# Input tiles stored tile-major and rope tables packed, with the tiles' loads queued behind slabs that they no longer block

## The chip, the cores and the metric

The kernel runs on the 8 cores of one Trainium2 chip, one batch element per core, with no traffic between cores. The time is device microseconds of the slowest core, lower is better. Executions fall into a fast and a slow state: in a slow run the cores of one die, or of both, show a lower granted TensorE clock (about 0.97 is usual) and take longer.

## The reference, cut to what matters

Four layers of a diffusion backbone over 2048 latent tokens and 256 context tokens, width 1024. Only the beginning matters: layer 0 normalises the input, modulates it by shift and scale vectors that come from one vector of conditioning, and feeds the pooling and attention mixer.

```python
for l in range(DEPTH):
    mod = silu_c @ w_mod[l] + b_mod[l]                  # 1024 x 6144: twelve slabs of 512 columns
    sh1, sc1, g1, sh2, sc2, g2 = [m[:, None, :] for m in jnp.split(mod, 6, axis=-1)]
    ...
    hx = modulate(rms_norm(x, norm1_g[l]), sh1, sc1)    # needs slabs 0 to 3
    if l % 2 == 0:
        ...                                             # k, v, q (rotated by the rope tables), pooling input u
        out_x, out_c = even_mixer(hx, hc, ...)
    else:
        ...                                             # conformer convolution
    x = x + g1 * out_x                                  # needs slabs 4 and 5
    x = x + g2 * sq_relu_mlp(modulate(rms_norm(x, norm2_g[l]), sh2, sc2), mlp_w1[l], mlp_w2[l])
    ...                                                 # slabs 6 to 11; the context stream likewise
```

## The kernel before

The tokens are worked on in five tiles: tiles 0 to 3 of 512 latent tokens, tile 4 with the 256 context tokens. The residual stream X stays in SBUF as float32, channels on partitions. Weights come in slabs of 1024 rows or columns through four slots (`WR`), loaded from the POOL queue, which also casts float32 to bfloat16 (a modulation slab's rows are 16 KB in the input, its packets in the trace 8192 B); the input tiles and rope tables are loaded from the SP queue, without a cast. Every engine's program is a list made at build time; each instruction waits for the semaphores of what it reads and of what it overwrites.

```python
X = SB("X", [128, 8, NT], F32)            # channel-major: the 512 tokens of one chunk of 128 channels, then the next
...
def dmas(self, qname, chan, pairs, reads=(), writes=()):
    q = self.E[qname]
    self._emit_waits(q, self._deps(chan, reads, writes))
    for (out, in_) in pairs:
        chan.count += 16
        q.q.append(("op", "dma_start", (), {"out": out, "in_": in_}, chan.sem, 16))
    self._record(chan, chan.count, reads, writes)       # a reader of a slot: the slot's next load waits for it
...
def load_x(tile, after=()):
    (t0, n, s, ti) = tile
    Sd.dma("sp", Sd.chan("x%d" % ti), X[:, :, t0:t0 + n],
           xP[:, 8 * t0:8 * (t0 + n)].rearrange("p (c t) -> p c t", c=8), reads=after, writes=xk(ti))
...
def pump():                               # loads the next slabs of the plan into slots that are free
    while slabs["free"] and slabs["next"] < len(plan):
        i = slabs["next"]
        slot = slabs["free"].pop(0)
        src, nk = plan[i]
        Sd.dma("pool", Sd.chan("w%d" % slot), WR[slot][:, 0:src.shape[1]], src, writes=[("W", slot)])
        ...
```

So that the tiles do not all load at once, a tile's load names a modulation slab in `reads`: it is issued when that slab has landed. A side effect is that the slot counts as read by the tile's transfer, and that the slot's next slab is not loaded before the tile has landed. The start of the program, and the part of the mixer where layer 0's slabs are used:

```python
X5 = x_tiles(True)
load_x(X5[0])
mods = [get_slab(w_mod[0, j], 8) for j in range(4)]
Sd.dma("pool", Sd.chan("ident"), IDB[:, :], identd, writes=[("c", "idb")])
first_mixer = even_mixer(0, X5, ...)      # issues rope table 0, X tile 1 behind slab 2, table 1, tile 2 behind slab 3,
                                          # table 2, tile 3, table 3, tile 4; two DMAs to a table, cosine and sine
for j in range(4):
    mod_slab(0, j, mods[j])               # 32 matmuls, then the slot is given back; from j = 1 on also tile 0's norm
    ...
for tile in X5[1:]:
    push_norm(0, 0, tile, ...)            # squares, statistics and pieces, run a few at a time between other work
...
kvs = get_slab(w_kv[i2], 8); qs_ = get_slab(w_q[i2], 8); us_ = get_slab(w_u[i2], 8)
kv_tile(all5[0], kvs, ...)                # key and value of tile 0
kv_tile(all5[1], kvs, ...)                # of tile 1, once its norm is done
for f in q_items(0, qs_):                 # queries of tile 0, with tile 2's norm between them
    f(); step(2)
kv_tile(all5[2], kvs, ...)
for b in range(4):
    u_item(b, us_); step(3)
mod_slab(0, 4)                            # then tile 3, slab 5, tile 4, slab 6; slabs 7 to 11 in the first attention
...
```

The softmax here doesn't subtract the row's maximum and nothing guards it: scores larger than these inputs give would overflow.

Of the kernel before, what the change touches and what calls it, by code (L numbers as in the profile page):

```python
# [14 lines left out]
NT = S + L  # L15
# [18 lines left out]
class Sched:  # L34
# [86 lines left out]

    def dma(self, qname, chan, out, in_, reads=(), writes=()):
        self.dmas(qname, chan, [(out, in_)], reads, writes)

    def dmas(self, qname, chan, pairs, reads=(), writes=()):
        if self.dry:
            return
        q = self.E[qname]
        self._emit_waits(q, self._deps(chan, reads, writes))
        for (out, in_) in pairs:  # L130
            chan.count += 16
            q.q.append(("op", "dma_start", (), {"out": out, "in_": in_}, chan.sem, 16))
        self._record(chan, chan.count, reads, writes)
# [108 lines left out]
def build():  # L242
# [22 lines left out]
    masksd = din("masks", [128, 2 * 128])  # L265
    ropec = din("ropec", [128, NT])
    ropes = din("ropes", [128, NT])
    permd = din("permc", [128, 128])
# [3 lines left out]
    with ExitStack() as st:  # L272
        def SB(name, shape, dt):
            return st.enter_context(nc.sbuf_tensor(name, shape, dt))

        X = SB("X", [128, 8, NT], F32)
        H = SB("H", [128, 8, NT], BF16)
# [26 lines left out]
        def emit(Sd, plan):  # L304
            dry = Sd.dry
            A = Arena(ART, ARENA_W, Sd)
            psk = lambda i: ("ps", i)
            hk = lambda ti: [("H", ti, c) for c in range(8)]
            xk = lambda ti: [("X", ti, c) for c in range(8)]

# [74 lines left out]
            def load_x(tile, after=()):  # L385
                (t0, n, s, ti) = tile
                Sd.dma("sp", Sd.chan("x%d" % ti), X[:, :, t0:t0 + n], xP[:, 8 * t0:8 * (t0 + n)].rearrange("p (c t) -> p c t", c=8),
                       reads=after, writes=xk(ti))

# [38 lines left out]
            def norm_sq(tile, c, k=2):  # L428
                (t0, n, s, ti) = tile
                ACT(H[:, c:c + k, t0:t0 + n], X[:, c:c + k, t0:t0 + n], AF.Square, [("X", ti, q) for q in range(c, c + k)],  # L430
                    [("H", ti, q) for q in range(c, c + k)])
# [12 lines left out]
            def norm_piece(lb, nrm, tile, r, c, mode="da"):  # L444
                (t0, n, s, ti) = tile
                tb = c % 2
                rst, rk, ak = RST[:, r, 0:n], ("rst", r), ("ab", lb, nrm, c // 2)
                tmp, x, h = TMP[:, tb, 0:n], X[:, c, t0:t0 + n], H[:, c, t0:t0 + n]
                if mode == "da":
# [23 lines left out]
            def push_final(tile, outb, sq=True):  # L473
# [8 lines left out]
                def piece(c):  # L482
                    STT(ob[:, c, 0:n], X[:, c, t0:t0 + n], vec("fing", c, c + 1), RST[:, r, 0:n], ALU.mult, ALU.mult,
                        [("X", ti, c), ("rst", r)] + VK, [ok[c]])
                    if c % 2:
                        Sd.dma("sp", Sd.chan("o%d%d" % (ti % 2, c // 2)), outP[:, 8 * t0 + (c - 1) * n:8 * t0 + (c + 1) * n].rearrange("p (c t) -> p c t", c=2),
                               ob[:, c - 1:c + 1, 0:n], reads=ok[c - 1:c + 1])
# [3 lines left out]
            def mlp_phase(l, tiles, next_l, next_tiles):  # L491
# [25 lines left out]
                def stage2(w2s, it, last):  # L517
                    (t0, n, s, ti) = tiles[it]
                    hb, hbk = hid[it % 2]
                    for oc in range(8):  # L520
                        pb = dbank()
                        for kk in range(4):
                            MM(PS[pb][:, 0:n], w2s[0][:, kk, oc * 128:(oc + 1) * 128], hb[:, kk, 0:n], kk == 0, kk == 3,
                               reads=[w2s[1], hbk[kk]], writes=[psk(pb)], last=(kk == 3))
                        STT(X[:, oc, t0:t0 + n], PS[pb][:, 0:n], gate(1, oc, s), X[:, oc, t0:t0 + n], ALU.mult, ALU.add,
                            [psk(pb), gkey(1, oc), ("X", ti, oc)], [("X", ti, oc)])
                        if last and ti in next_ti and oc % 2:
                            norm_sq(tiles[it], oc - 1)
                        step()
# [24 lines left out]
            def proj_item(slabs_, tile, oc):  # L554
# [3 lines left out]
                for k in range(8):  # L558
                    MM(PS[pb][:, 0:n], sl[0][:, k, (oc % 4) * 128:(oc % 4 + 1) * 128], H[:, k, t0:t0 + n], k == 0, k == 7,
                       reads=[sl[1], ("H", ti, k)], writes=[psk(pb)], last=(k == 7))  # L560
                STT(X[:, oc, t0:t0 + n], PS[pb][:, 0:n], gate(0, oc, s), X[:, oc, t0:t0 + n], ALU.mult, ALU.add,
                    [psk(pb), gkey(0, oc), ("X", ti, oc)], [("X", ti, oc)])
# [165 lines left out]

            def even_mixer(l, tiles, loads=()):
                i2 = l // 2  # L730
# [7 lines left out]
                Qs = [A.bf16("Qs%d" % i, 4, 512, parts=4) for i in range(2)]  # L738
                Us = [A.bf16("Us%d" % i, 512) for i in range(NU_)]
                Pb = [A.bf16("P%d" % i, 1024) for i in range(NP)]  # L740
                Db = [A.bf16("Db%d" % i, 512) for i in range(2)]
                BND, Bk = A.bf16("BND", 20, 128)
                MSK, Mk = A.bf16("MSK", 2, 128)
                PW, PWk = A.bf16("PW", 4, 128)
                RT = [(A.f32("rc%d" % i, 512), A.f32("rs%d" % i, 512)) for i in range(2)]
                t1, t1k = A.f32("t1", 512)
# [12 lines left out]
                def rope_buf(i):  # L759
                    if i < 2:  # L760
                        return RT[i]
                    return tuple((Pb[2 * i - 4 + j][0].bitcast(F32), Pb[2 * i - 4 + j][1]) for j in range(2))

                def load_rope(ti, i):
                    t0, n = all5[ti][0:2]
                    (rc, rck), (rs, rsk) = rope_buf(i)
                    Sd.dmas("sp", Sd.chan("rt%d" % i), [(rc[:, 0:n], ropec[:, t0:t0 + n]), (rs[:, 0:n], ropes[:, t0:t0 + n])], writes=rck + rsk)

                def rope_a(pq, tab, n):
                    (rc, rck), (rs, rsk) = tab  # L770
                    ub = UB[cnt["u"] % 2]
                    cnt["u"] += 1
                    TT(t1[:, 0:n], PS[pq][:, 0:n], rc[:, 0:n], ALU.mult, [psk(pq)] + rck, t1k)
                    TT(ub[0][:, 0:n], PS[pq][:, 0:n], rs[:, 0:n], ALU.mult, [psk(pq)] + rsk, ub[1])
                    return ub
# [155 lines left out]
                def even_run():  # L931
# [3 lines left out]
                    qs_ = get_slab(w_q[i2], 8)  # L935
                    us_ = get_slab(w_u[i2], 8)
                    Sd.dma("pool", Sd.chan("c0"), BND[:, :, :], bandsd.rearrange("p (a b) -> p a b", a=20), writes=Bk)
                    Sd.dma("pool", Sd.chan("c2"), PW[:, :, :], pool_w[i2].rearrange("g c d -> c g d"), writes=PWk)
# [52 lines left out]

                for i in range(4):
                    load_rope(i, i)
                    if loads:
                        loads[i]()
                return even_run
# [4 lines left out]
            Sd.dma("pool", Sd.chan("ident"), IDB[:, :], identd, writes=[("c", "idb")])  # L1001
            first_mixer = even_mixer(0, X5, [(lambda t_, a_: (lambda: load_x(t_, a_)))(X5[i + 1], [mods[min(i + 2, 3)][1]]) for i in range(4)])
            r = next_rst()
# [86 lines left out]
def _prep_shared(inp):  # L1090
# [52 lines left out]
    sh["masks"] = masks  # L1143
    sh["ropec"] = rc
    sh["ropes"] = rs
    return {k: np.ascontiguousarray(v, dtype=np.float32) for k, v in sh.items()}, vecs
# [23 lines left out]
```

## Time and profile before

| | |
|---|---|
| time | 3360.4 us median of four runs, the three fast ones 3358.7 to 3361.1 (one slow run of 3580) |
| profiled run | fast; cores 3340.7 to 3359.7 us, granted clock 0.967 to 0.972 |
| X tiles 0, 1, 2, 3 landed (mean of the 8 cores) | 37.5, 56.2, 71.1, 79.0 us |
| matmuls of slab 4, of slab 11 start (mean of the 8 cores) | 105.6, 163.2 us |

The landing times come from the trace's records of when each transfer's semaphore reached its full count; the others from the lists of instructions. In the views PE is TensorE (PEld its weight loads), DVE VectorE, ACT ScalarE, POOL GpSimd, and SP SyncE, which here only issues transfers; `psa` is PSUM, `wr` a slab's slot, `H` the normalised tile. First the page of the slowest core: its busy times, and the busy tenths of TensorE and of the DMA engines in 40 equal slices of 84 us.

```profile
span 3359.7 us, 44105 instructions; the slowest of 8 cores (3340.7 to 3359.7 us)
...
PE 3069.6 (91%) x18180; PEld 1414.6 (42%) x18180; DVE 1883.1 (56%) x2957; ACT 1221.4 (36%) x1796; POOL 76.4 (2%) x147
...
PE   3688899999989879999998888999999988899997
...
DMA  9710132342224622323332101225241362222212
...
```

TensorE is the bottleneck, at 91%, but the first two slices read 3 and 6 where the rest reads 8 and 9, while the DMA engines read 9 and 7. Only the start has something to give. The same by windows, with the mean granted clock, the DMA share and GB/s that landed in the last three columns:

```profile
...
core 1: us, PE busy (x) PEld busy (x) DVE busy (x) ACT busy (x) POOL busy (x), PEclk, DMA share, GB/s
0.00:40.00 40.00, 2.54 (x66) 2.00 (x66) 1.24 (x9) 4.65 (x6) 5.10 (x13) 1.00 0.94 185
40.00:100.00 60.00, 40.55 (x256) 18.75 (x255) 36.41 (x63) 28.11 (x36) 2.34 (x4) 0.83 0.92 225
100.00:200.00 100.00, 67.20 (x586) 31.71 (x584) 36.25 (x73) 39.38 (x58) 4.76 (x9) 0.78 0.59 102
...
```

The chain of waits in order of time, for the slowest core: start, length, and what the end of the program was waiting for then.

```profile
...
2.73 28.72 DMA wr<-w_mod
...
31.47 25.16 DMA X<-xP
...
70.71 8.75 PE psa L144 x51
...
99.51 8.30 PE psa L144 x66
...
108.09 9.63 DMA wr<-w_mod
...
```

Slabs until 31.5, then X tile 1, which is issued when slab 2 has landed and lands at 56.6; then tile 1's norm, tile 2's, the u blocks at 99.5 to 107.8, and from 108 on the slabs that load one by one. The timeline of ACT shows when each tile's squares could begin (the last bracket is the idle time before, and what ended it):

```profile
...
38.34 3.90 ACT L144 ACTIVATE H<-X 128x1024 bf16<-128x1024 f32 x4 [32.95 <-DMA X<-xP]
...
56.66 1.06 ACT L144 ACTIVATE H<-X 128x1024 bf16<-128x1024 f32 x1 [3.53 <-DMA X<-xP]
...
71.53 2.01 ACT L144 ACTIVATE H<-X 128x1024 bf16<-128x1024 f32 x2 [0.87 <-DMA X<-xP]
...
```

And the POOL queue, which issues the slabs:

```profile
...
57.16 0.53 POOL L144 DMA_DIRECT2D wr<-w_u  x1 [30.29 <-DMA X<-xP]
85.00 0.53 POOL L144 DMA_DIRECT2D wr<-w_mod  x1 [27.31 <-DMA X<-xP]
...
```

The slot of slab 2 is given back near 44 us, that of slab 3 near 50, when their matmuls are done, but w_u is issued at 57.2, when tile 1 has landed, and slab 4 at 85.0, when tile 4 has. Last, three lines of TensorE's timeline, the 32 short matmuls each of slabs 4, 5 and 11.

```profile
...
106.85 0.94 PE L144 MATMUL psa<-SC,wr 128*128 128x2 bf16 x32
...
117.86 0.94 PE L144 MATMUL psa<-SC,wr 128*128 128x2 bf16 x32 [2.48 <-DMA wr<-w_mod]
...
167.15 0.94 PE L144 MATMUL psa<-SC,wr 128*128 128x2 bf16 x32 [1.37 <-DMA wr<-w_mod]
...
```

Slab 4 has no bracket: it was used without a wait, in spite of its late issue. Each slab after it is waited for, since its load starts only when a slot comes free.

### The profile page before, as it was taken

The page shows a single profiled execution, that of the slowest core. Times are in us where ns is not written, and L with a number is a line of the kernel's source. Part 1 is how long each engine was busy: PE and PEld are TensorE (multiplying, and loading weights), DVE is VectorE, ACT ScalarE, POOL GpSimd, SP SyncE. Part 2 cuts the span into 40 slices and gives each one's busy share as a digit, 9 for nine tenths or more (in the row PEclk, how much of TensorE's full clock was granted, in tenths as well). Part 3 has the DMA queues.
Part 4 walks back from the last instruction along what each step waited for, and adds up shares of the span by engine and source line. Part 5 has one row for each costly group of instructions (what it writes and reads, how often), then busy time and mean ns, then how long its engine had stood idle before and what let it go on. Part 6 is the DMA issues. An engine that isn't in the chain of part 4 may idle for free.

```text
span 3359.7 us, 44105 instructions; the slowest of 8 cores (3340.7 to 3359.7 us)
## 1 busy us (share of the span) xinstructions
PE 3069.6 (91%) x18180; PEld 1414.6 (42%) x18180; DVE 1883.1 (56%) x2957; ACT 1221.4 (36%) x1796; POOL 76.4 (2%) x147
## 2 busy tenths in 40 slices
PE   3688899999989879999998888999999988899997
PEld 1333354554444334545544332444443433344443
DVE  3444466666652466666656444666666335766666
ACT  3366531111352576111126456311116247511113
POOL 0000000000000000000000000000000000000000
PEclk9799899999999999999999998999999999999999
DMA  9710132342224622323332101225241362222212
GB/s 222 124 24 1 26 56 51 76 76 51 51 55 101 153 65 51 73 53 71 68 57 36 26 1 27 51 51 100 51 92 40 78 159 73 38 38 38 38 26 101
DMA packets 87913, 215.54 MB, mean 64 GB/s; under 512 B 13344, under 2 KB 61088, under 8 KB 70816
## 3 DMA queue, kind: packets, MB, share of 16 engines
q0 software_dynamic: 21360, 141.25, 23.0%
q1 hardware_dynamic: 66352, 71.47, 7.8%
q8 instruction: 143, 2.34, 0.3%
q14 instruction: 58, 0.48, 0.0%
HBM read 336.36 MB, written 17.56 MB: 105 GB/s over the span
## 4 chain that ended last, share of the span: by engine, by line
PE 74%; DVE 12%; ACT 8%; DMA 4%; issue 2%; SPq 0%; DVEq 0%; POOL 0%; ACTq 0%; POOLq 0%
PE psa L144 74%; DVE ARENA L144 5%; ACT H L144 4%; ACT ARENA L144 4%; DVE TMP L144 3%; DMA wr<-w_mod 2%; DVE X L144 2%; DMA ARENA<-gscr 1%; DMA X<-xP 1%; ACT L144 1%; DVE H L144 1%; ACT RST L144 0%; SPq L144 0%; DVE MODV L144 0%; POOL wr L144 0%
## 5 line engine op out<-in xcount | busy, mean ns | idle before, releaser
L144 PE MATMUL psa<-H,wr 128*128 128x512 bf16 (+1 forms) x7280 | 1580.0, 374 | 71.8 <-ACT H L144 29.5
L144 ACT ACTIVATE ARENA<-psa 128x512 f32<-128x512 f32 (+3 forms) x895 | 580.8, 653 | 1632.7 <-PE psa L144 1602.3
L144 PEld LDWEIGHTS psa<-H,wr 128*128 128x128 bf16 x7280 | 707.8, 99 | 889.6 <-issue 63.5
L144 DVE SCALAR_TENSOR_TENSOR X<-psa,MODV,X 128x512 f32<-128x512 f32 (+1 forms) x1296 | 902.9, 717 | 163.4 <-PE psa L144 102.6
L144 PE MATMUL psa<-ARENA,wr 128*128 128x512 bf16 (+1 forms) x4608 | 965.6, 368 | 0.0
L144 DVE TENSOR_TENSOR ARENA<-ARENA 128x512 bf16<-128x512 f32 (+4 forms) x789 | 522.1, 664 | 765.3 <-ACT ARENA L144 762.8
L144 PEld LDWEIGHTS psa<-ARENA,wr 128*128 128x128 bf16 x4608 | 452.7, 98 | 491.1 <-issue 4.4
L144 PE MATMUL psa<-ARENA 128*32 128x512 bf16 (+5 forms) x3404 | 321.4, 374 | 78.6 <-ACT ARENA L144 46.4
L144 ACT ACTIVATE H<-TMP,AB 128x512 bf16<-128x512 f32 (+1 forms) x276 | 189.4, 693 | 251.1 <-DVE TMP L144 251.1
L144 PEld LDWEIGHTS psa<-ARENA 128*32 128x32 bf16 (+3 forms) x3404 | 120.3, 100 | 301.3 <-issue 137.0
L144 DVE TENSOR_TENSOR ARENA<-psa,ARENA 128x512 bf16<-128x512 f32 (+2 forms) x186 | 122.2, 677 | 217.3 <-PE psa L144 189.7
L144 DVE SCALAR_TENSOR_TENSOR TMP<-X,AB,RST 128x512 f32<-128x512 f32 (+1 forms) x276 | 193.5, 708 | 44.6 <-ACT RST L144 43.9
L144 ACT ACTIVATE H<-X 128x1024 bf16<-128x1024 f32 (+1 forms) x164 | 160.9, 999 | 75.2 <-DVE X L144 37.8
L144 PE MATMUL psa<-H,ONES 128*128 128x512 bf16 (+1 forms) x472 | 131.7, 391 | 59.9 <-ACT H L144 53.9
L144 PE MATMUL psa<-SC,wr 128*128 128x2 bf16 x1536 | 45.9, 164 | 59.5 <-DMA wr<-w_mod 50.1
L144 DVE CAST H<-ARENA 128x512 bf16<-128x512 f32 (+1 forms) x72 | 29.7, 412 | 123.9 <-ACT ARENA L144 123.9
L144 PE MATMUL psa<-wr,H 128*128 128x128 bf16 (+1 forms) x560 | 88.6, 317 | 9.8 <-DVE ARENA L144 9.8
L144 PEld LDWEIGHTS psa<-H,ONES 128*128 128x128 bf16 x472 | 40.4, 99 | 134.1 <-ACT H L144 78.9
L144 POOL DMA_DIRECT2D wr<-w x64 | 33.8, 529 | 2032.1 <-PE psa L144 2032.1
L144 PEld LDWEIGHTS psa<-SC,wr 128*128 128x128 bf16 x1536 | 43.9, 97 | 69.6 <-issue 40.4
L144 ACT ACTIVATE H<-ARENA,VEC 128x512 bf16<-128x512 f32 (+1 forms) x72 | 55.9, 789 | 42.3 <-DVE ARENA L144 41.9
L144 ACT ACTIVATE ARENA<-psa,VEC 128x512 f32<-128x512 f32 (+1 forms) x72 | 46.8, 651 | 61.3 <-PE psa L144 61.3
(43 smaller groups left out, 568.2 us busy)
## 6 DMA issues: line engine op xcount, KB each, us to landing
wr<-w POOLq DMA_DIRECT2D x64, 1024.0 KB, 8.6
wr<-w_mod POOLq DMA_DIRECT2D x48, 1024.0 KB, 8.1
ARENA<-gscr SPq DMA_DIRECT2D x256, 135.0 KB, 3.0
wr<-pw POOLq DMA_DIRECT2D x12, 1024.0 KB, 8.0
gscr<-ARENA SPq DMA_DIRECT2D x65, 128.0 KB, 1.8
X<-xP SPq DMA_DIRECT2D x4, 2048.0 KB, 29.2
outP<-ARENA SPq DMA_DIRECT2D x16, 512.0 KB, 2.7
wr<-w_out POOLq DMA_DIRECT2D x4, 1024.0 KB, 9.2
```

The costliest lines, as they stand in the source:

```text
L144: ins = getattr(e, it[1])(*it[2], **it[3])
```

## The change

The intent is to take the input tiles out of the way of the weights: tiles as 128 rows of 16 KB instead of 1024 runs of 2 KB, rope tables as one transfer of 4 KB rows instead of two of 2 KB rows, and a wait (`after`) that orders a tile behind a slab without making it a reader of the slot. Tile 1 now waits for slab 3, tile 2 for the key/value slab, tiles 3 and 4 for the query slab. The core of the diff (helper lines, the other uses of `X[:, c, ...]` and the preparation on the host cut):

```diff
-    def dmas(self, qname, chan, pairs, reads=(), writes=()):
+    def dmas(self, qname, chan, pairs, reads=(), writes=(), after=()):
...
-        self._emit_waits(q, self._deps(chan, reads, writes))
+        self._emit_waits(q, self._deps(chan, list(reads) + list(after), writes))
...
-        X = SB("X", [128, 8, NT], F32)
+        X = SB("X", [128, 8 * NT], F32)
...
+            xv = lambda t0, n: X[:, 8 * t0:8 * (t0 + n)].rearrange("p (c t) -> p c t", c=8)
...
-                Sd.dma("sp", Sd.chan("x%d" % ti), X[:, :, t0:t0 + n], xP[...].rearrange("p (c t) -> p c t", c=8),
-                       reads=after, writes=xk(ti))
+                Sd.dma("sp", Sd.chan("x%d" % ti), X[:, 8 * t0:8 * (t0 + n)], xP[:, 8 * t0:8 * (t0 + n)],
+                       writes=xk(ti), after=after)
...
-                    Sd.dmas("sp", Sd.chan("rt%d" % i), [(rc[:, 0:n], ropec[:, t0:t0 + n]), (rs[:, 0:n], ropes[:, t0:t0 + n])], writes=rck + rsk)
+                    Sd.dma("sp", Sd.chan("rt%d" % i), tab, roped[ti], writes=tk)
...
                     us_ = get_slab(w_u[i2], 8)
+                    if xs:
+                        load_rope(1, 1)
+                        load_rope(2, 2)
+                        load_x(xs[2], [kvs[1]])
+                        load_rope(3, 3)
+                        load_x(xs[3], [qs_[1]])
+                        load_x(xs[4], [qs_[1]])
...
-                for i in range(4):
-                    load_rope(i, i)
-                    if loads:
-                        loads[i]()
+                load_rope(0, 0)
...
-            first_mixer = even_mixer(0, X5, [(lambda t_, a_: (lambda: load_x(t_, a_)))(X5[i + 1], [mods[min(i + 2, 3)][1]]) for i in range(4)])
+            first_mixer = even_mixer(0, X5, X5)
+            load_x(X5[1], [mods[3][1]])
```

More of the change, by code (lines that the diff above doesn't have):

```diff
@@ L120, in mm, with dma @@
         self._record(eng, cnt, reads, writes)
-    def dma(self, qname, chan, out, in_, reads=(), writes=()):
-        self.dmas(qname, chan, [(out, in_)], reads, writes)
-    def dmas(self, qname, chan, pairs, reads=(), writes=()):
+    def dma(self, qname, chan, out, in_, reads=(), writes=(), after=()):
+        self.dmas(qname, chan, [(out, in_)], reads, writes, after)
+    def dmas(self, qname, chan, pairs, reads=(), writes=(), after=()):
         if self.dry:
@@ L265, in build @@
     masksd = din("masks", [128, 2 * 128])
-    ropec = din("ropec", [128, NT])
-    ropes = din("ropes", [128, NT])
+    roped = din("rope", [4, 128, 1024])
     permd = din("permc", [128, 128])
@@ L386, in load_x @@
                 (t0, n, s, ti) = tile
-                Sd.dma("sp", Sd.chan("x%d" % ti), X[:, :, t0:t0 + n], xP[:, 8 * t0:8 * (t0 + n)].rearrange("p (c t) -> p c t", c=8),
-                       reads=after, writes=xk(ti))
+                Sd.dma("sp", Sd.chan("x%d" % ti), X[:, 8 * t0:8 * (t0 + n)], xP[:, 8 * t0:8 * (t0 + n)],
+                       writes=xk(ti), after=after)
             def zero_pads():
@@ L429, in norm_sq @@
                 (t0, n, s, ti) = tile
-                ACT(H[:, c:c + k, t0:t0 + n], X[:, c:c + k, t0:t0 + n], AF.Square, [("X", ti, q) for q in range(c, c + k)],
+                ACT(H[:, c:c + k, t0:t0 + n], xv(t0, n)[:, c:c + k, :], AF.Square, [("X", ti, q) for q in range(c, c + k)],
                     [("H", ti, q) for q in range(c, c + k)])
@@ L447, in norm_piece @@
                 rst, rk, ak = RST[:, r, 0:n], ("rst", r), ("ab", lb, nrm, c // 2)
-                tmp, x, h = TMP[:, tb, 0:n], X[:, c, t0:t0 + n], H[:, c, t0:t0 + n]
+                tmp, x, h = TMP[:, tb, 0:n], xv(t0, n)[:, c, :], H[:, c, t0:t0 + n]
                 if mode == "da":
@@ L482, in piece @@
                 def piece(c):
-                    STT(ob[:, c, 0:n], X[:, c, t0:t0 + n], vec("fing", c, c + 1), RST[:, r, 0:n], ALU.mult, ALU.mult,
+                    STT(ob[:, c, 0:n], xv(t0, n)[:, c, :], vec("fing", c, c + 1), RST[:, r, 0:n], ALU.mult, ALU.mult,
                         [("X", ti, c), ("rst", r)] + VK, [ok[c]])
@@ L524, in stage2 @@
                                reads=[w2s[1], hbk[kk]], writes=[psk(pb)], last=(kk == 3))
-                        STT(X[:, oc, t0:t0 + n], PS[pb][:, 0:n], gate(1, oc, s), X[:, oc, t0:t0 + n], ALU.mult, ALU.add,
+                        STT(xv(t0, n)[:, oc, :], PS[pb][:, 0:n], gate(1, oc, s), xv(t0, n)[:, oc, :], ALU.mult, ALU.add,
                             [psk(pb), gkey(1, oc), ("X", ti, oc)], [("X", ti, oc)])
@@ L560, in proj_item @@
                        reads=[sl[1], ("H", ti, k)], writes=[psk(pb)], last=(k == 7))
-                STT(X[:, oc, t0:t0 + n], PS[pb][:, 0:n], gate(0, oc, s), X[:, oc, t0:t0 + n], ALU.mult, ALU.add,
+                STT(xv(t0, n)[:, oc, :], PS[pb][:, 0:n], gate(0, oc, s), xv(t0, n)[:, oc, :], ALU.mult, ALU.add,
                     [psk(pb), gkey(0, oc), ("X", ti, oc)], [("X", ti, oc)])
@@ L727, in conv_mixer, with even_mixer @@
                 push_norm(lb, 1, tiles[T - 1], ("n2", tiles[T - 1][3]))
-            def even_mixer(l, tiles, loads=()):
+            def even_mixer(l, tiles, xs=()):
                 i2 = l // 2
@@ L739, in even_mixer @@
                 Us = [A.bf16("Us%d" % i, 512) for i in range(NU_)]
+                po = A.off
                 Pb = [A.bf16("P%d" % i, 1024) for i in range(NP)]
+                PT = [(ART[:, po + 1024 * i:po + 1024 * (i + 1)], Pb[2 * i][1] + Pb[2 * i + 1][1]) for i in range(2)]
                 Db = [A.bf16("Db%d" % i, 512) for i in range(2)]
@@ L744, in even_mixer @@
                 PW, PWk = A.bf16("PW", 4, 128)
-                RT = [(A.f32("rc%d" % i, 512), A.f32("rs%d" % i, 512)) for i in range(2)]
+                RT = [A.f32("rt%d" % i, 1024) for i in range(2)]
                 t1, t1k = A.f32("t1", 512)
@@ L759, in rope_buf @@
                 def rope_buf(i):
-                    if i < 2:
-                        return RT[i]
-                    return tuple((Pb[2 * i - 4 + j][0].bitcast(F32), Pb[2 * i - 4 + j][1]) for j in range(2))
+                    return RT[i] if i < 2 else PT[i - 2]
                 def load_rope(ti, i):
-                    t0, n = all5[ti][0:2]
-                    (rc, rck), (rs, rsk) = rope_buf(i)
-                    Sd.dmas("sp", Sd.chan("rt%d" % i), [(rc[:, 0:n], ropec[:, t0:t0 + n]), (rs[:, 0:n], ropes[:, t0:t0 + n])], writes=rck + rsk)
+                    tab, tk = rope_buf(i)
+                    Sd.dma("sp", Sd.chan("rt%d" % i), tab, roped[ti], writes=tk)
                 def rope_a(pq, tab, n):
-                    (rc, rck), (rs, rsk) = tab
+                    tab, tk = tab
                     ub = UB[cnt["u"] % 2]
                     cnt["u"] += 1
-                    TT(t1[:, 0:n], PS[pq][:, 0:n], rc[:, 0:n], ALU.mult, [psk(pq)] + rck, t1k)
-                    TT(ub[0][:, 0:n], PS[pq][:, 0:n], rs[:, 0:n], ALU.mult, [psk(pq)] + rsk, ub[1])
+                    TT(t1[:, 0:n], PS[pq][:, 0:n], tab[:, 0:n], ALU.mult, [psk(pq)] + tk, t1k)
+                    TT(ub[0][:, 0:n], PS[pq][:, 0:n], tab[:, 512:512 + n], ALU.mult, [psk(pq)] + tk, ub[1])
                     return ub
@@ L990, in even_run @@
                     push_norm(lb, 1, tiles[T - 1], ("n2", tiles[T - 1][3]))
-                for i in range(4):
-                    load_rope(i, i)
-                    if loads:
-                        loads[i]()
+                load_rope(0, 0)
+                if not xs:
+                    for i in range(1, 4):
+                        load_rope(i, i)
                 return even_run
@@ L1143, in _prep_shared @@
     sh["masks"] = masks
-    sh["ropec"] = rc
-    sh["ropes"] = rs
+    sh["rope"] = np.stack([np.concatenate([r[:, i * 512:(i + 1) * 512] for r in (rc, rs)], axis=1) for i in range(4)])
     return {k: np.ascontiguousarray(v, dtype=np.float32) for k, v in sh.items()}, vecs
```

## The prediction

> **What bounds the kernel.** TensorE is busy 3069.6 us of 3359.7 (91%, the page's busy times). No matmul changes, and DVE and ACT instructions keep their shapes (X updates 717 ns), so after 200 us I expect nothing. The start can move: TensorE is busy 2.5 us of the first 40, 40.6 of the next 60, 67.2 of the next 100 (busy time by windows).
>
> **What bounds the start** (chain in order of time). Slabs until 31.5; X tile 1 lands at 56.6; its norm until 70.7; X tile 2 (landed about 71.5), its norm interleaved with the query rotation on DVE until 92; key/value of tile 2; slab 4 at 106.9; from there to 167 seven more slabs, 9 to 14 us of loading each through one or two free slots. DMA is full from 3 to 84 us, about 0.34 MB/us of HBM reads (slabs are read as float32, twice what lands).
>
> **What the change does.**
> 1. X packets become 16 KB, not 2 KB; rope packets 4 KB, not 2. [...] 54 slab and 60 X packets per 3 us at 18 to 36 us. So X gets about half of the bytes. Tile 0 should land at 14 to 17 us, not 38; slabs 0 to 3 still end near 38. Tile 0's norm ends near 42, not 53.5.
> 2. Tile 1 now waits for slab 3 (38, not 31.5) but shares fairly: from packet durations (0.74 us a slab packet, as much for 16 KB of X) I estimate landing at 50 to 53, not 56.6.
> 3. w_u no longer waits for tile 1 (issue about 33, was 57.2), nor slab 4 for tile 4 (about 40, was 85.0). Neither was waited for: slab 4 was used at 106.9 without a wait. But these 4.2 MB now go packet for packet with the rope tables and tile 2. About 25 MB are read before tile 2 lands: at 0.34 MB/us plus 4 us that is 77 us, not 71.5.
> 4. SP's issues, up to 13 us long (SP timeline), fall below 1 us; nothing waited on them.
>
> **On the critical path.** Tile 1 gains 4 us; tile 2 loses about 6, of which some 2 come back because its squares then run without a gap. Slab 4's matmul moves from 106.9 to 108 to 111; the slab chain behind it is unchanged. Alone: +1 to +4 us. [...] Together +1 us.
>
> **Prediction:** 3362 us, 8 times in 10 between 3353 and 3371 (fast state). Faster by over 2%: 0.01; within 2%: 0.97; slower by over 2%: 0.02.
>
> **What the profile would show.** Packets of 16384 B in the hardware queue. First squares near 16 us, not 38.3. w_u issued near 33, slab 4 near 40. Tile 2's squares at 75 to 79. Slab matmuls 5 to 11 with the same waits, shifted by one constant. Windows after 300 us equal.
>
> **What would make it wrong.** If the queue cuts rows smaller, tiles 1 and 2 land later: worse. If reads reach 0.36 MB/us, tile 2 comes before 72 and 3 to 6 us are gained. If slab 4 is not what gates 107 to 167, the early slots gain more.

The counts are measured: on core 1 of the kernel before, 321 slab packets and 361 packets of X and rope tables from 18 to 36 us. That X then gets half of the bytes was the estimate from these counts. The second was a term of the sum: up to 4 us of gain, for a higher rate of reading that no trace had shown, set against the +1 to +4 us. With it the sum came to the +1 us that "Together" gives; without it, it is the +1 to +4.

## The result, and the profile after

The changed kernel took 3371.3 us median (3369.1 to 3372.3, four runs, all fast), against 3360.4 before. The ratio is 1.0033 with a 95% interval of 1.0014 to 1.0053. A ratio here is the mean time of one kernel's fast runs over that of the other's fast runs of the same rounds, so not quite the ratio of the medians. The interval leaves no doubt that it is slower, by about 11 us, and the time lies 0.3 us outside the predicted range. A second measurement, in later rounds, gave 3368.4 against 3358.7 (means of fast runs).

The views of before, for the changed kernel. Its slowest core in the profile is core 3. The page:

```profile
span 3367.5 us, 44087 instructions; the slowest of 8 cores (3354.1 to 3367.5 us)
...
PE 3061.8 (91%) x18180; PEld 1412.8 (42%) x18180; DVE 1883.2 (56%) x2957; ACT 1222.5 (36%) x1796; POOL 76.4 (2%) x147
...
PE   3688899999989888999997888999999988899997
...
DMA  9520132442224622333432101336352363122212
...
```

```profile
...
core 3: us, PE busy (x) PEld busy (x) DVE busy (x) ACT busy (x) POOL busy (x), PEclk, DMA share, GB/s
0.00:40.00 40.00, 6.41 (x104) 3.77 (x104) 7.25 (x21) 10.38 (x13) 5.64 (x14) 1.00 0.96 182
40.00:100.00 60.00, 31.90 (x167) 13.30 (x168) 25.67 (x43) 17.19 (x22) 1.80 (x3) 0.73 0.85 220
100.00:200.00 100.00, 69.85 (x604) 34.67 (x602) 38.33 (x77) 38.96 (x56) 4.76 (x9) 0.75 0.60 106
...
```

In the first 40 us TensorE does more (6.4 us, was 2.5), in the next 60 it does less (31.9, was 40.6). The chain of waits:

```profile
...
21.13 22.92 DMA wr<-w_kv
...
44.07 37.72 DMA X<-xP
...
107.97 8.30 PE psa L145 x66
...
116.56 9.58 DMA wr<-w_mod
...
```

Tile 2 stands where tile 1 stood: it is issued at 44.1, when the key/value slab has landed, and lands at 81.8. The u blocks that were at 99.5 are at 108.0. The squares on ACT:

```profile
...
16.07 3.90 ACT L145 ACTIVATE H<-X 128x1024 bf16<-128x1024 f32 x4 [10.14 <-DMA X<-xP]
...
58.38 1.06 ACT L145 ACTIVATE H<-X 128x1024 bf16<-128x1024 f32 x1 [14.28 <-DMA X<-xP]
...
81.81 2.00 ACT L145 ACTIVATE H<-X 128x1024 bf16<-128x1024 f32 x2 [9.43 <-DMA X<-xP]
...
```

Tile 0's squares begin at 16, not 38. Tile 1's begin at 58.4, 1.7 us later than on core 1 before. Tile 2's begin at 81.8 after 9.4 us of idle time. The slabs' issue on POOL, and the matmuls of slabs 4, 5 and 11:

```profile
...
34.70 0.53 POOL L145 DMA_DIRECT2D wr<-w_u  x1 [5.17 <-PE psa L145]
42.24 0.53 POOL L145 DMA_DIRECT2D wr<-w_mod  x1 [7.01 <-PE psa L145]
...
```

```profile
...
115.32 0.94 PE L145 MATMUL psa<-SC,wr 128*128 128x2 bf16 x32
...
126.28 0.99 PE L145 MATMUL psa<-SC,wr 128*128 128x2 bf16 x32 [2.42 <-DMA wr<-w_mod]
...
175.24 0.95 PE L145 MATMUL psa<-SC,wr 128*128 128x2 bf16 x32 [0.78 <-DVE ARENA L145]
...
```

w_u is issued at 34.7 and slab 4 at 42.2, as intended. Slab 4 landed at 71.5 (mean of the cores) and lay unused until 115.

What the DMA engines did is best read from one window. First the kernel before, core 1, up to 71.5 us, when its tile 2 landed; the columns are packets, MB landed, and share of the engines' time; q0 carries what POOL issues, mostly slabs, q1 what SP issues, mostly X and rope tables:

```profile
...
q0 software_dynamic: 1440, 6.92, 55.9%
q1 hardware_dynamic: 4231, 8.26, 41.0%
...
```

The same window of the changed kernel, core 1 again:

```profile
...
q0 software_dynamic: 1636, 8.24, 66.6%
q1 hardware_dynamic: 890, 6.37, 31.4%
...
```

The slabs are read as float32 and land as bfloat16, so a slab's MB counts twice at HBM (over the whole run twice q0's 141.25 MB and q1's 71.47 make 354.0; the page gives 336.4 MB read and 17.6 written). From the trace's packet records on that basis, core 1 had read 22.1 MB by 71.5 us before and 22.6 MB after, 2% more. But 1.3 MB more of slabs had landed, and 1.9 MB less of X and tables. Large packets did not slow the engines; the bytes came in another order.

### The profile page after: what moved, and what is told of

Its sections match the earlier page's. It is cut to its first block, busy times and chain, and to the rows that moved or that the text cites. A ratio compares the mean times of both kernels' runs of the same rounds, so it can differ in the third digit from the quotient of the medians.

```text
span 3367.5 us, 44087 instructions; the slowest of 8 cores (3354.1 to 3367.5 us)
## 1 busy us (share of the span) xinstructions
PE 3061.8 (91%) x18180; PEld 1412.8 (42%) x18180; DVE 1883.2 (56%) x2957; ACT 1222.5 (36%) x1796; POOL 76.4 (2%) x147
## 3 DMA queue, kind: packets, MB, share of 16 engines
q0 software_dynamic: 21360, 141.25, 24.8%
q1 hardware_dynamic: 60144, 71.47, 7.6%
## 4 chain that ended last, share of the span: by engine, by line
PE 43%; issue 39%; DVE 7%; ACT 5%; DMA 5%; POOL 1%; SPq 0%; DVEq 0%; POOLq 0%; ACTq 0%
PE psa L145 43%; DVE ARENA L145 4%; ACT ARENA L145 3%; ACT H L145 2%; DMA wr<-w_mod 2%; DVE TMP L145 2%; DVE X L145 1%; DMA X<-xP 1%; POOL wr L145 1%; DMA wr<-w_kv 1%; DMA ARENA<-gscr 1%; DVE H L145 0%; DMA ARENA<-permc 0%; ACT L145 0%; ACT RST L145 0%
## 5 line engine op out<-in xcount | busy, mean ns | idle before, releaser
L145 ACT ACTIVATE H<-ARENA,VEC 128x512 bf16<-128x512 f32 (+1 forms) x72 | 56.1, 792 | 42.3 <-DVE ARENA L145 41.9
L145 ACT ACTIVATE ARENA<-psa,VEC 128x512 f32<-128x512 f32 (+1 forms) x72 | 46.9, 652 | 64.9 <-PE psa L145 64.9
## 6 DMA issues: line engine op xcount, KB each, us to landing
wr<-w POOLq DMA_DIRECT2D x64, 1024.0 KB, 10.1
```

The source lines that it names most:

```text
L145: ins = getattr(e, it[1])(*it[2], **it[3])
```

## The experiments

**Theory A** is the one of the prediction: the DMA engines are full until 84 us (busy share 0.97 to 0.99 from 3 to 84 us on the 8 cores of the kernel before), and take packets from the two queues in turn (on core 1 there 321 of q0 and 361 of q1 from 18 to 36 us, 308 to 324 and 361 to 443 on all cores). What counts is what goes ahead of X tiles 1 and 2 and of the slabs that their work needs. **Rival B**: the new layout costs time by itself, by large packets or by X's new place in SBUF. **Rival C**: unblocked slots are good as such. **Rival D**: the slabs' use does not matter, only tile 2's chain. All edits were correct against the reference. The times are means of the fast runs of up to five rounds and a profiled run, beside the kernel before on the same chip (there were two chips: before took 3362.7 and 3362.2 on one, 3358.7 on the other).

| run | fast runs, mean (before) | ratio, 95% interval | tile 1, tile 2 land | slab 4, slab 11 used |
|---|---|---|---|---|
| the change, again | 3368.4 (3358.7) | 1.0029, 1.0015 to 1.0042 | 57.2, 81.9 | 114.7, 172.5 |
| layout only | 3373.3 (3362.7) | 1.0032, 1.0017 to 1.0046 | 46.8, 60.6 | 115.1, 173.7 |
| unblocking only | 3381.7 (3362.7) | 1.0057, 1.0042 to 1.0071 | 74.3, 83.6 | 123.5, 181.7 |
| slabs held | 3364.7, two runs (3362.7) | none | 57.0, 66.3 | 106.7, 165.4 |
| slabs held, again | 3362.7 (3362.2) | 1.0002, 0.9986 to 1.0018 | 57.1, 66.9 | 106.5, 164.7 |
| ropes behind tile 2 | 3366.4 (3362.7) | 1.0011, 0.9995 to 1.0027 | 58.1, 70.5 | 111.4, 169.3 |
| early use of slabs | 3369.2 (3358.7) | 1.0035, 1.0007 to 1.0063 | 56.6, 81.8 | 75.0, 158.8 |
| X first | 3355.5 (3358.7) | 0.9990, 0.9971 to 1.0009 | 46.9, 62.8 | 97.0, 153.5 |
| X first, again | 3356.4 (3362.2) | 0.9982, 0.9969 to 0.9995 | 49.2, 64.8 | 99.0, 157.0 |
| X first, not held | 3361.8 (3362.2) | 0.9998, 0.9982 to 1.0014 | 46.7, 70.1 | 103.1, 162.0 |
| X first and early use | 3360.2 (3358.7) | 1.0004, 0.9991 to 1.0018 | 48.4, 63.4 | 82.2, 151.7 |

The last two columns are microseconds in the profiled run, means of the 8 cores (before: 56.2, 71.1; 105.6, 163.2).

### The change again

The changed kernel, unedited.

> The changed kernel itself, unedited, to have it on the same chip and in the same rounds as the three edits beside it. Both theories: 8 to 12 us slower than before, X tile 2's squares at 80 to 83 us and slab 4 at 114 to 116, as in its first profile.

Measured: 9.7 us slower than before; slab 4 at 113.5 to 115.6. As expected, and the reference for what follows.

### The layout alone

```diff
-                       writes=xk(ti), after=after)
+                       writes=xk(ti), reads=after)
...
+                for i in range(4):
+                    load_rope(i, i)
+                    if xs:
+                        load_x(xs[i + 1], [mods[min(i + 2, 3)][1]])
```
(and the change's own order of loads removed)

> The change's layout alone (tile-major X, packed rope tables, so 16 KB and 4 KB packets), with the order of issue and the blocking of slots as before. Theory A (packets take turns, so what counts is how many slab bytes go ahead of X tiles 1 and 2; large packets only raise X's share): tile 1 lands near 46, tile 2 near 62 us, not 56.6 and 71.5; modulation slab 4 is used near 98 to 101, not 106.9; the kernel gains 4 to 8 us on before. Rival B (large packets or the new place of X in SBUF cost time by themselves): no gain on before, or the 10 us of the changed kernel's loss stay.

Measured: the tiles land as expected, at 46.8 and 60.6, but slab 4 is used at 115.1, not at 98 to 101, and the kernel is 10.6 us slower. By its time rival B wins here. TensorE's timeline, core 1, says what was waited for.

```profile
...
41.50 0.99 PE L145 MATMUL psa<-SC,wr 128*128 128x2 bf16 x32 [6.39 <-DMA wr<-w_mod]
61.01 3.57 PE L145 MATMUL psa<-H,wr 128*128 128x512 bf16 x8 [18.52 <-DMA wr<-w_kv]
...
```

It waited 18.5 us for the key/value slab, which landed at 61.5 (mean of the cores; 46.1 before), and the query slab landed at 73.1 (53.0 before). The turn-taking works in both directions. Four X tiles in large packets were in the SP queue, and each packet of the other queue let one of them pass: three small tables of 8 to 64 KB that stand ahead of the key/value slab, and landed by 42 us before, landed at 47, 50 and 56. I had counted only what the slabs take from X. So large packets in this order do cost time, through the turns and not by a slower rate (core 1 had read 22.1 MB by 71.5 us, as before); whether the layout costs anything without such an order is tested below, with the slabs held.

### The unblocked slots alone

```diff
-                       reads=after, writes=xk(ti))
+                       writes=xk(ti), after=after)
```
(in the kernel before, with `after` added to `dma` and `dmas` as in the change)

> The unblocked slots alone: X tiles are waited for as before, in 2 KB packets and in the order of before, but w_u and slab 4 no longer wait for X tiles 1 and 4. Theory A: w_u, slab 4 and the bands then go one packet to one 2 KB packet of X, so tile 1 lands near 75 us, not 56.6; slab 4 is used near 122 to 126; the kernel loses 14 to 20 us on before, more than the whole change. Rival B (layout costs): within 2 us of before. Rival C (unblocking is good as such): faster than before.

Measured: tile 1 lands at 74.3, slab 4 is used at 123.5, the kernel loses 19 us. All as theory A has it. Tile 1's squares, ACT, core 1 (56.66 before):

```profile
...
73.89 1.06 ACT L144 ACTIVATE H<-X 128x1024 bf16<-128x1024 f32 x1 [20.93 <-DMA X<-xP]
...
```

Rival C is refuted: the unblocking costs more than the whole change. Since there is no new layout here, a loss needs none; that the layout adds nothing of its own is not shown by this run. The 2 KB packets of X get about one turn for each 8 KB packet of a slab (361 to 321 on core 1 of the kernel before, 18 to 36 us), so with the two extra slabs queued tile 1 waits until they are through (w_u landed at 61.3 and slab 4 at 68.3).

### The slabs held until tile 2 has landed

```diff
-                while slabs["free"] and slabs["next"] < len(plan):
+                while slabs["free"] and slabs["next"] < min(len(plan), slabs["cap"]):   # cap: 6 until tile 2 is queued
...
-                    Sd.dma("pool", ..., src, writes=[("W", slot)])
+                    Sd.dma("pool", ..., src, writes=[("W", slot)], after=xk(2) if i == 6 else ())
```

> The changed kernel, but w_u, and with it slab 4, the bands and the pooling weights behind it on the same queue, are issued only when X tile 2 has landed. Theory A: tile 2 lands at 64 to 67 us, not 81.4; its squares wait for tile 1's norm again; slab 4 is used at 104 to 107, not 115; the loss of the change goes: within 3 us of before. Rival B: the loss of 10 us stays, as the layout stays.

> The held slabs again, unedited, since only two of its runs were fast. Theory A: the ten microseconds of the change stay gone: mean of the cores' spans on undisturbed dies within 2 us of before, time within 4 us. Rival B (the layout costs): at least 5 us slower than before.

Only two runs of the first were fast, so it was repeated: 1.0002, with slab 4 at 106.5. The whole loss is gone while the layout stays: the mean span of the cores on undisturbed dies was 3353.9, against 3353.5 of the kernel before in the same rounds (in the first run 3353.7 against 3353.7). This refutes rival B for the change. What was held is w_u and slab 4, with the bands and pooling weights (tables of the pooling mixer) queued behind them. ACT's timeline, core 1 of the repeat:

```profile
...
57.17 1.06 ACT L145 ACTIVATE H<-X 128x1024 bf16<-128x1024 f32 x1 [13.91 <-DMA X<-xP]
...
70.76 1.99 ACT L145 ACTIVATE H<-X 128x1024 bf16<-128x1024 f32 x2
...
```

Tile 2's squares follow tile 1's norm at 70.8 with no wait for X. The landings show the size of a turn. In the changed kernel rope table 1 lands 8.0 us after tile 1 (65.2 after 57.2), table 2 another 7.0 after, tile 2 9.8 after that; with the slabs held, first run, it is 1.4, 1.4 and 6.5 us. Of the 15 us that tile 2 gains, the path takes 8.5, since tile 1's norm then ends last.

### The rope tables behind tile 2

```diff
+                        load_x(xs[2], [kvs[1]])
                         load_rope(1, 1)
                         load_rope(2, 2)
-                        load_x(xs[2], [kvs[1]])
```

> The changed kernel with the rope tables 1 and 2 issued behind X tile 2, not ahead of it; slots and layout as changed. Theory A, in its packet form: a rope table's 8 packets of 4 KB per engine let 8 slab packets pass, some 7 us each, so tile 2 lands at 66 to 69 us, not 81.4, although only 1 MB was moved behind it; slab 4 is used at 106 to 109; within 3 us of before. In its byte form (only bytes ahead count), tile 2 gains 3 us: lands near 78, slab 4 near 112. Rival B: no change from the changed kernel.

Measured: tile 2 lands at 70.5, 11.5 us earlier than in the change, though only 1 MB was moved behind it. At 0.34 MB/us that megabyte is worth 3 us, so the packet form of theory A holds and the byte form does not: a table of 8 packets of 4 KB per engine (128 rows on 16 engines) lets 8 slab packets go ahead. The change's profile has the turns: from 57 to 72 us 250 packets of q0, mostly slabs, and 255 of q1, mostly rope tables, on core 1; 250 to 268 and 255 to 268 on the 8 cores (packets over 64 B). Tile 2's squares, ACT, core 1, again follow tile 1's norm with no wait for X:

```profile
...
72.26 1.99 ACT L145 ACTIVATE H<-X 128x1024 bf16<-128x1024 f32 x2
...
```

Slab 4 came at 111.4, later than the 106 to 109 expected, and the time was 3.7 us over before, not within 3. I had forgotten table 1, which now landed at 78.0: DVE waited 5.8 us for it on core 1 (4.5 to 5.8 on cores 0 to 3) before it could rotate tile 1's keys.

### Slabs used early in the changed kernel

```diff
                     kv_tile(all5[1], kvs, rope_buf(1), 2)
+                    mod_slab(0, 4)
                     for f in q_items(0, qs_): ...
                     need(("n1", 2))
+                    mod_slab(0, 5)
                     kv_tile(all5[2], kvs, rope_buf(2), 2)
                     for b in range(4): ...
-                    mod_slab(0, 4)
+                    mod_slab(0, 6)
```
(and slabs 5 and 6 removed from where they were; each `if l == 0`)

> The changed kernel with every transfer as changed, but the matmuls of slab 4 moved up to right after tile 1's key/value, where TensorE waits for X tile 2, those of slab 5 to before tile 2's key/value, and those of slab 6 to after the first four u blocks; slabs 7 to 11 as before, in the first attention. Theory A: the early landing of slab 4 (70 us) was worth nothing only because its use stayed at 115; slab 4 is used at 77 to 81, slab 5 at 98 to 101, slab 6 at 114 to 117, slab 11 at 155 to 163 and not at 168 to 177; 12 to 18 us faster than the changed kernel, so 2 to 8 us faster than before. Rival D (the start is bound by X tile 2 and the chain behind it alone; where the slabs are used does not matter): as the changed kernel, within 3 us.

Measured: the slabs are used as expected, 4 at 75.0, 11 at 158.8, 14 us earlier than in the change. Yet the time is 3369.2 and the interval wide. The windows of two cores of the profiled run, 110 to 270 us (the third value from the end is the mean granted clock):

```profile
core 0 of [0, 1, 2, 3, 4, 5, 6, 7], span 3363.6 us
...
110.00:270.00 160.00, 138.14 (x866) 53.89 (x865) 65.59 (x115) 77.94 (x105) 3.72 (x7) 0.77 0.30 51
...
```

```profile
core 2 of [0, 1, 2, 3, 4, 5, 6, 7], span 3342.8 us
...
110.00:270.00 160.00, 130.46 (x932) 55.10 (x948) 72.60 (x126) 85.87 (x116) 3.70 (x7) 0.94 0.29 50
...
```

Core 0, and core 1 with it, got a clock of 0.77 where core 2 got 0.94. The trace's clock records show why: between 109 and 270 us cores 0 and 1 were granted 0.8125 wherever they were not at one half; cores 2 to 7 never. Cores 2 to 7 ended 0.7 us under their spans of before (mean), after leading by 5.4 at 440 us; cores 0 and 1 ended 6.4 us over theirs. So on the undisturbed cores the early use gains back most of the change's loss (it ends 9.7 us over on the mean of all cores of the unedited change), and rival D is refuted for the start. On the time of the slowest core the 2 to 8 us of gain that were expected did not show: in three of the four fast runs the slowest core had a mean clock of 0.961 to 0.965, and the fourth run, with no core under 0.968, took 3360.0, about as before.

### X first

Tile 1 behind slab 2, with its squares, statistics and first pieces ahead of tile 0's key/value; tile 2 right behind the key/value slab, its table after it; w_u, slab 4, bands and the small tables only when tile 2 has landed.

```diff
                 load_rope(0, 0)
+                if xs:
+                    load_x(xs[1], [mods[2][1]])
+                    load_rope(1, 1)
...
                     if xs:
-                        load_rope(1, 1)
-                        load_rope(2, 2)
                         load_x(xs[2], [kvs[1]])
-                        load_rope(3, 3)
+                        load_rope(2, 2)
                         load_x(xs[3], [qs_[1]])
+                        load_rope(3, 3)
                         load_x(xs[4], [qs_[1]])
+                    # now identity and masks, which stood ahead of the key/value slab; w_u and slab 4 held as above
...
+                    step(9)
-                    kv_tile(all5[0], kvs, rope_buf(0), 1)
+                    kv_tile(all5[0], kvs, rope_buf(0), 2)
```

> The new layout with an order that serves the critical path: X tile 1 behind slab 2, its squares and statistics ahead of tile 0's key/value; X tile 2 behind the key/value slab; w_u, slab 4, the bands and the small tables only after X tile 2 has landed. Slabs are used where they were. Theory A: tile 1 lands near 46, tile 2 near 63, slab 4 is used at 95 to 99, slab 11 at 156 to 161; 5 to 11 us faster than before. Rival B (the layout costs): not faster than before.

> The order that serves X first again, unedited. In undisturbed runs: 6 to 10 us faster than before (3350 against 3359), slab 4 at 94 to 99. If the 13/16 clock that the first profile showed on cores 6 and 7 from 51 to 251 us is an accident of that run, no core shows it again; if the fuller start brings it, some runs have cores at a mean clock under 0.9655 and 10 to 15 us longer, which the kernel before has not shown in a fast run.

The first time it had only three fast runs, and one of them (3365.4, the profiled one) shows 0.8125 on cores 6 and 7 between 51 and 251 us; the other two took 3350.6 and 3350.4 (cores 4 and 5 of that profile also met 0.8125, from 3287 us on). Repeated: five fast runs of 3353.3 to 3358.5, ratio 0.9982 (0.9969 to 0.9995), no 0.8125 in its profile and no pair of cores at a low clock in its runs. The squares on ACT, core 1 of the repeat:

```profile
...
48.16 3.90 ACT L145 ACTIVATE H<-X 128x1024 bf16<-128x1024 f32 x4 [2.82 <-DMA X<-xP]
...
64.62 2.00 ACT L145 ACTIVATE H<-X 128x1024 bf16<-128x1024 f32 x2 [1.15 <-DMA X<-xP]
...
```

Tile 1 at 48.2 and tile 2 at 64.6, with waits of 2.8 and 1.2 us for X. Slab 4 follows at 99.0. This version beats both kernels, by 5.8 us or 0.2% against before (6 to 10 were expected) and, going by the two ratios to before (0.9982 and 1.0029 to 1.0033), by about 0.5% against the change.

### X first, slabs not held

The same without the two edits of `pump`.

> As the run before it, but w_u, slab 4, the bands and the small tables are issued as soon as a slot is free, as the change has it. It tells what the hold is worth when tile 2 is no longer behind the rope tables. Theory A, packet form: X tile 2's 8 packets per engine pass against 8 slab packets, so tile 2 lands 3 to 5 us later than with the hold, at 66 to 69; slab 4 is used at 98 to 102; 3 to 7 us faster than before. If any unblocking costs the 10 us of the change: tile 2 at 75 or later and no gain on before.

Measured: tile 2 at 70.1 instead of 64.8, slab 4 at 103.1 instead of 99.0, no gain on before left (0.9998). So the hold is worth some 4 us at slab 4, and 5 in time, even where tile 2 stands ahead of the tables. The landing was a microsecond later than expected, and the time did not gain the 3 to 7 us I had written.

### X first and early use

X first, with slab 4 ahead of w_u in the plan and used before tile 2's key/value, slab 5 after the first u blocks, slab 6 after tile 4's key/value.

> As the run before it, with slab 4 loaded ahead of w_u and used before tile 2's key/value, slab 5 after the first four u blocks, slab 6 after the context tile's key/value, whose slot is given back before it. Theory A, both halves: slab 4 at 80 to 86, slab 5 at 95 to 99, slab 6 at 106 to 112, slab 11 at 140 to 150; 14 to 25 us faster than before, the fastest of all.

A miss. Slab 4 at 82.2 and slab 11 at 151.7, somewhat later than expected, but the time is that of before, 1.0004. In the profiled run the four cores of die 0 were granted 0.8125 between 111 and 273 us. Those of die 1 were not, and lay 12.1 us under their spans of before at 440 us and 5.7 under at the end. That is what "X first" without early use has on its undisturbed cores (11.9 and 6.3 in its first profile, cores 0 to 5), so the early use adds nothing there either. The trace shows where the head start goes: slab 4 is used 14.8 us earlier than in that profile (82.2, was 97.0), but slab 5, issued at 83.6, lands only at 102.2, TensorE waits 5 to 6 us for it on six of the cores, and slab 6 is used at 115.3 (was 116.3), slab 11 at 151.7 (was 153.5). The slabs from 6 on, which load one by one, gain 1 to 2 us.

## Why the prediction was wrong

The time was 0.3 us outside the range. The mechanism and its sign were right: w_u and slab 4 now go ahead of the tables and of tile 2, and slab 4 is used later. Its size was not: +1 us was said, +10 to +11 came. **The step that failed is the landing of tile 2.** The sum on the critical path took it from a count of bytes, 77 us and 6 later than before; it landed at 82.0, 10.9 later.

- **After 200 us, nothing.** Held. The mean lag of the 8 cores was 9.2 us at their first update of X near 203 us, and 10.1 at the end.
- **Packets of 16 KB, tile 0 at 14 to 17 us, norm of tile 0 done near 42.** Held: 512 packets of 16384 B in the first 100 us (core 1), landing at 16.1 (mean), the norm's last piece on ACT at 41.2 to 41.9 on core 1. Slab 3 landed at 39.9, not 38.
- **Tile 1 lands at 50 to 53, gains 4 us.** Missed. It landed at 57.2, 1.0 us later than before. It is issued when slab 3 has landed, 39.9, not 38, and on core 0 the engines carry rows of the key/value and query slabs until its first packets start near 45. These then run at about 0.8 us each, in turn with query slab packets of 0.74 to 0.8: 8 pairs are 12 to 13 us. The prediction had started the clock at 38 and taken 0.74 for both. Tile 1 is not on the path any more, but the tables and tile 2 stand behind it in the SP queue.
- **Tile 2 lands at 77, loses 6.** The step that failed. It lost 10.9 us (82.0 after 71.1). The count said 25 MB at 0.34 MB/us plus 4 us. By 81.4 us, when its tile 2 landed, core 1 had read 25.9 MB. And the loss of 6 set a calculated 77 against a measured 71.5: the same formula gives 69.0 for the kernel before, with the 22.1 MB that core 1 had read. With the measured bytes on both sides it gives a loss of 3.8 / 0.34 = 11.2 us (an estimate; 9.9 measured on that core). The 0.34 was high, too: past the first 4 us these counts are 0.327 MB/us before and 0.335 after. Counted in packets, too, it is the 57.2 of tile 1, two tables of 8.0 and 7.0 us, and 9.8 us for tile 2.
- **Some 2 us come back, since the squares run without a gap.** Held: on core 1 the squares began 9.9 us later and the statistics were ready 7.4 us later.
- **Slab 4 at 108 to 111.** It was 115.1 (mean), 9.5 us later than before. Tile 2's 10.9 us less the 2.5 that came back make 8.4; the last microsecond is not accounted for.
- **The slab chain behind is unchanged.** Held on the mean: from slab 4 to slab 11 57.6 us before and after. Single cores changed by up to 7 us (the last section says how).
- **Neither w_u nor slab 4 had been waited for, so their early issue gains nothing.** Held, and the run of early use shows what it would take: an earlier use.
- **A higher rate and up to 4 us of gain.** Hardly happened (on core 1 22.1 MB before and 22.6 after by 71.5 us, 2% more), and gained nothing. It was a hope, not worked out from a trace, and I subtracted it from a mechanism that I had costed, which turned +1 to +4 into +1; with tile 2's loss costed on both sides the sum would have been near 9 (11.2 less 2.5, an estimate).
- **SP's issues fall below 1 us, and nothing waited on them.** Held: 0.3 to 0.6 us each on core 3, where they took up to 13.8 before.

What the runs showed beyond that: the loss is that of the turns of w_u, slab 4 and what is queued behind them, ahead of tables and tile 2, all of it (slabs held: 1.0002). Unblocking alone costs 19 us; the rest of the change, large packets and the new order of loads together, gives 9 back. Large packets alone, in the old order, cost 10.6 us, by starving the key/value slab.

Settled by runs: what costs the 10 us, and that the layout does not in the order of the change. Open: the 0.8125 clock. Of the 13 profiles it stands near the start in three, all with a fuller start (early use, X first, X first and early use), but not in the other two of X first. That the fuller start brings it is not shown: an untested rival is a short spell of the slow state, which every kernel has in some executions (two to five of the runs of each row of the table), and which a run counted as fast can hide when it is short.

## What to carry to other kernels

Here two queues shared full DMA engines packet by packet (250 to 268 packets against 255 to 268 in 15 us), and a table of 8 packets per engine took about 8 times one packet of each queue (0.75 and 0.2 us, so 7.6 us as an estimate; 7.0 and 8.0 measured): so a small table cost the time of a large slab's packets, and removing a false dependency lets bytes in ahead of those that someone else waits for. Before freeing a prefetch, ask who waits for what it will overtake, and when it will be used; hold it until the transfer on the critical path has landed. A gain at the start must be followed to the end of the slowest core, because another core or the clock can take it back (in the early-use run cores 0 and 1 got a clock of 0.77 and 0.78, the others 0.93 to 0.96).

## What the traces show of the queues, the pairs of cores and the clock

- **Turns.** The packets of the two queues come in similar numbers at three pairs of sizes. At 8192 B of a slab to 2048 B of X and rope tables: 308 to 324 against 361 to 443 from 18 to 36 us of the kernel before (8 cores). At 8192 to 16384 of X: 93 to 113 against 99 to 110, and 16 to 33 of the first rope table, from 4 to 16 us of the change. At 8192 to 4096 of rope tables, with some of 5120 and 16384: 250 to 268 against 255 to 268 from 57 to 72 us. What follows when the sizes differ: a table of 0.5 MB took 7.0 to 8.0 us beside slab packets and 1.4 us without them, and SP's queue got 12 to 15% of the bytes read in the first of these windows, about half (49 to 55%) in the second (a slab's packet reads 16 KB and lands 8).
- **Packets.** The trace's packet records are of 8192 B for slabs (software queue; 4096 B for the key/value slab) and of 16384 B for X (hardware queue; 2048 B before), each one row of the transfer.
- **Pairs of cores.** The core that is ahead gets through the slabs faster: from slab 4 to slab 11 core 0 took 55.2 us and core 1 60.3 before, 61.3 and 53.2 after the change, where core 1 was ahead. In 47 of the 48 pairs (cores 0 and 1, 2 and 3, and so on) of the 12 profiles other than "X first and early use" the core that used slab 4 first took less, and in each of the 12 the slowest core was the one of its pair that was behind at slab 11. What the two cores of a pair share, no trace shows.
- **The 0.8125 clock.** In one profile all four cores of die 0 had it (from 111 us on), in a second only cores 0 and 1, in a third only 6 and 7 early on. It ended by 251 to 273 us while the matmuls went on (in the first, from 280 us to the end, die 0 had a mean clock of 0.98 with TensorE busy 2857 to 2883 of 3082 us). The kernel before, TensorE 91 to 92% busy on the 8 cores, has no such record on any core in its fast profile, nor has the change: all are 1.0 or 0.5. In slow runs the mean clocks went down to 0.80, but no trace of one was kept.
